# Where a pooled branch is split into high and low parts: in SBUF by two engines, or as it leaves PSUM and by way of HBM

## The chip, the cores and the metric

The kernel runs on one core of a Trainium2 chip. The metric is the device time in microseconds (us) of one execution. TensorE (PE) multiplies matrices and writes to PSUM, VectorE (DVE) and ScalarE (ACT) work on tiles in SBUF and PSUM, GpSimd (POOL) on tiles in SBUF; SyncE (SP) does no arithmetic and starts transfers. A transfer can be started from SP's queue or from POOL's.

## What is computed

One block of a streaming encoder over 16 meta tokens and 1024 tokens of width 1024. Of the reference, what matters here:

```python
a, q, k, v, r, lr, ga, gb = jnp.split(rmsnorm(h, norm_mix) @ w_in, IN_SPLITS, axis=-1)
p = multiscale_pool(a).reshape(B, L, 4, 128)            # trailing means of 2, 4, 8, 16 tokens, less the token
p = jnp.einsum('blgc,gce->blge', p, w_pool_mix).reshape(B, L, 512) * pool_scale
y_a = p @ w_pool_out                                    # 512 -> 1024
log_a = log_sigmoid(lr @ w_gate_up + b_gate) / 16       # lr: 16 columns
o = gla_chunked(q, k, v, log_a)                         # chunks of 64 tokens, 4 heads, state 64 x 128
y_b = (rmsnorm(o) * silu(r)) @ w_gla_out
h = h + (sigmoid(ga) * y_a + sigmoid(gb) * y_b) @ w_out
h = h + squared_relu_mlp(rmsnorm(h))                    # 1024 -> 4096 -> 1024, then a last rmsnorm
```

## The kernel before

All products are float32. A float32 matrix is kept as two float32r parts: the high part is a rounded copy, the low part is the matrix less its high part. `mm3` (L251) then issues three matmuls, high by high (L255), high by low (L256) and low by high (L257). Activations lie transposed, channels on the partitions and tokens along the free axis, in two halves of 512 tokens; `TH[h]` and `TL[h]` are the high and low parts of the normalised input of half h. Weights come through rings of slots: `W1` (L59 to L89) loads 512 KB of raw weights from HBM by SP (L110), ACT writes the high part (L83) and `W1.eng` the low part (L87). That engine is DVE at first and POOL from `gla_open` on, where a slot is split in four quarters of 256 columns.

The stages, with their times in the profiled execution: the gates and other projections up to 245 us, the pooling stage 245 to 304 us, the GLA stage 304 to 475 us, then the merge and `w_out`, then the MLP to the end.

**Pooling stage.** For each of four groups g of 128 channels, `a_block` projects the input, `mean_block` (L892) takes the trailing means on DVE and splits them (high by ACT L904, low by DVE L905), and `mix_block` (L909) multiplies by `w_pool_mix` and has ACT (L915) scale the result from PSUM into a float32 tile `pm` of all 1024 tokens. The steps stand in a list (L965): a of the next group stands between the mean and the mix of one. Then come the queries read back from HBM, the first block of keys `k_block(0)`, the mix of group 0, and `load_vw(1)`, which fetches and splits the second half of the weights of v (high ACT L471, low POOL L474).

**GLA stage.** `gla_open` (L988) gives SBUF and PSUM a new layout and calls `lr_of(0)`, which builds the stacked low-rank rows of the first half: a memset by POOL (L542), copies by ACT (L545) and a difference by DVE (L546), all in `stacked`. The stage walks through four units (token half, head pair): (0,0), (1,0), (0,1), (1,1). A unit starts with its log decay (L1180: PE L1183, ACT L1184 to L1187, DVE L1188), goes on to the running products (DVE L1261 to L1276, ACT L1254, L1257, L1273) and inside scores (PE L1240, L1243), and ends in `across` (L1310): PE L1329 multiplies keys by values, DVE L1335 chains eight states one after the other (W, last S) from these, PE L1342 and L1352 multiply into the states, PE L1370 transposes back. Between the pieces of a unit a list of fill work is poured into PE: k, v, the last two gate blocks, then the pooled product `ya_block` (L938) and the output product of the GLA branch. ya needs the pooled tile in two parts: `pooled_parts` (L1035), run during gate block 7 (`gb_last`, L1047), writes them over `TH[1]` and `TL[1]`, since block 7 is the last reader of these: 8 copies by ACT (L1041), 16 differences by POOL (L1043). Its eight steps come with the eight k steps of block 7's second token half. A gate block runs its halves in the order 1, 0, and a sigmoid of a half is ACT L923 to L925 and L1063 with DVE L926 in the middle.

**What sets the order.** PE's program is written by hand (L1803). The order of ACT, DVE, POOL and SP in these two stages is chosen by a scheduler that looks at the costs the program names; the engine then runs its queue strictly in order. A tile's next writer waits for its last reader.

Of the kernel before, what the change touches and what calls it, by code (L numbers as in the profile page):

```python
# [114 lines left out]
def kernel(  # L115
# [49 lines left out]
    q_dram = dp.tile([2, 2, P, HALF], F32, name="q_dram")  # L165
    r_dram = dp.tile([HEADS, 2, P, HALF], F32, name="r_dram")
    h_dram = dp.tile([8, P, D], F32, name="h_dram")
    hf_dram = [dp.tile([NPAIR, P, HALF], F32, name=f"hf{m}_dram") for m in range(7)]

    ident = left.push("ident", [P, P], F32)  # L170
# [256 lines left out]
    def drive(steps):  # L427

        for ring, aps, fn in steps:
            if fn not in (start, gate_stage):  # L430
                for r in rings:
                    r.top_up()
            wbs = [ring.views.pop(ring.done + ring.kept + i) for i in range(len(aps))] if ring else []
            held = len(aps)
            for cost in fn(*wbs) or ():
                if cost == "free":
                    ring.done, held = ring.done + held, 0
                    for r in rings:
                        r.top_up()
                elif cost == "keep":  # L440
                    ring.kept, held = ring.kept + held, 0
                else:
                    yield cost
            if ring:
                ring.done += held
# [19 lines left out]
    def load_vw(i, raws=None, parts=False):  # L465
        vw, raws = S["vw"][i], raws or fetch_vw(i)
        c = [slice(j * P, (j + 1) * P) for j in range(2)]
        eng = pool if i else dve

        def hi(j):  # L470
            act.activation(vw[:, 0, :, c[j]], raws[j], ACT.Copy)  # L471

        def lo(j):
            eng.tensor_tensor(vw[:, 1, :, c[j]], raws[j], f32(vw[:, 0, :, c[j]]), ALU.subtract)  # L474

        def lr():
# [383 lines left out]
    def pool_open():  # L860
        left.pop_to(left0)
        S["kq"] = [left.push(f"kq{h}", [P, 2, 2, HALF + OFF[h]], F32) for h in range(2)]
        S["left_k"] = left.mark()
        buffer("a", 2, SEQ + META)
        buffer("s", 2, SEQ + META)
        right.pop_to(0)
        S["vw"].append(right.push("vw1", [P, 2, KT, 256], F32R))
        S["pm"] = right.push("pm", [P, 4, SEQ], F32)
        S["ph"] = right.push("ph", [P, 2, SEQ], F32R)
        mw = S["mw"] = right.push("mw", [P, 2, 4, P], F32R)  # L870
        r = raw.load(w_pool_mix.rearrange("g c e -> c g e"), 4 * P).rearrange("p (g e) -> p g e", g=4)
# [37 lines left out]
    def mix_block(g):  # L909
        def fn():  # L910
            wb = (S["mw"][:, 0, g], S["mw"][:, 1, g])
            for tag, c in zip(("ms", "ms"), halves()):
                b = bank(tag)
                mm3(b, 1, lambda i: wb, lambda i: (S["ph"][:, 0, c], S["ph"][:, 1, c]))
                act.activation(S["pm"][:, g, c], b, ACT.Copy, scale=pscale[:, g : g + 1])  # L915
                yield

        return fn
# [19 lines left out]
    def ya_block(j):  # L938
        def fn(wb):
            hi, lo = (t.rearrange("p (k c) -> p k c", k=4) for t in wb)  # L940
            ph, pl = S["pm2"]
            for e, (h, c) in ((e, x) for e in range(2) for x in enumerate(halves())):
                b, w = bank("mm"), slice(e * P, (e + 1) * P)
                for k in (3, 2, 1, 0):
                    mm3(
                        b, 1, lambda i: (hi[:, k, w], lo[:, k, w]), lambda i: (ph[:, k, c], pl[:, k, c]),
                        first=k == 3, last=k == 0,
                    )
                    yield 3 * 512 / 2400
# [12 lines left out]
    a_ = lambda g: step(one, a_block(g), W1, [w_cols(C_A + g * P)])  # L962
    p_ = lambda g: step(one, mean_block(g))
    m_ = lambda g: step(one, mix_block(g))
    for f, i in (  # L965
        (a_, 3), (p_, 3), (a_, 2), (m_, 3), (p_, 2), (a_, 1), (m_, 2), (p_, 1), (a_, 0), (m_, 1), (p_, 0),
    ):
        f(i)

# [9 lines left out]
            for p in range(2):  # L979
                nc.sync.dma_start(q[:, p], q_dram[p, h])  # L980

    step(one, queries)
    step(one, k_block(0), W1, [w_cols(C_K)])
    m_(0)
    step(one, lambda: load_vw(1))


    def gla_open():  # L988
        raw.back()
        W1.eng = pool  # L990
        right.pop_to(2)
        left.pop_to(S["left_k"])
        S["v"].append(left.push("v1", [P, NC, 2 * P], F32))
        buffer("t1", 3)
# [22 lines left out]

    def v_second():
# [5 lines left out]
            leave()  # L1024

    def yg_open():
        S["yg"] = {0: S["vw"][1].rearrange("p n k c -> p (n k c)").rearrange("p (n h c) -> p n h c", n=2, h=HEADS)}

    def yg_last():
        right.pop_to(1)  # L1030
        S["yg"][1] = right.push("yg1", [P, 2, HEADS, HALF], F32R)
        done.add("pm")

    def pooled_parts():


        S["pm2"] = [a[1].rearrange("p k c -> p (k c)").rearrange("p (g c) -> p g c", g=4) for a in (TH, TL)]
        for c in halves():
            for g in (3, 2, 1, 0):
                (ph, pl), pm = (a[:, g, c] for a in S["pm2"]), S["pm"][:, g, c]  # L1040
                act.activation(ph, pm, ACT.Copy)  # L1041
                for q in halves_of_half:
                    pool.tensor_tensor(pl[:, q], pm[:, q], f32(ph[:, q]), ALU.subtract)  # L1043
                yield

    def gb_last(d):
        def fn(wb):  # L1047
            parts = pooled_parts()
            for n, cost in enumerate(gb_block(d, MAIN[::-1])(wb)):
                if n >= KT:  # L1050
                    next(parts, None)
                if n in (KT, KT + 1):
                    gate_load()
                yield cost

        return fn


    def gb_block(d, pieces=MAIN):
# [6 lines left out]
        return lambda wb: project(wb, pieces, evac)  # L1066

    staged = {}

# [240 lines left out]
    def across(p, half):  # L1310
# [38 lines left out]
        for j in (3, 0, 1, 2):  # L1349
            for e, u in ((0, 0), (1, 0), (1, 1), (0, 1)):  # L1350
# [493 lines left out]
```

## Time and profile before

| what | value |
|---|---|
| median of 3 executions | 1222.09 us (1220.26 to 1222.21) |
| the profiled execution | 1217.61 us |
| its span, from the first instruction to the last | 1215.8 us |
| PE busy | 1191.6 us, 98% of the span |
| VectorE busy | 869.7 us, 72% |
| ScalarE busy | 626.3 us, 52% |
| GpSimd busy | 75.0 us, 6% |
| granted TensorE clock | 0.998 |
| moved by DMA | 173.85 MB, 143 GB/s over the span |

A row of the timeline gives a start and a duration in us, the engine, the line, the operation, the tile written and the tiles read, shapes and a count; behind it in brackets how long the engine had been idle and what released it. Several like instructions in a row are one row, with the time of all. The list of waits gives for an engine what it waited for, in total, how often, and the longest. PE's matmuls overlap: one of 512 columns is shown at some 0.39 us and the next begins 0.23 us later.

### The profile page before, as it was taken

How to read it: one execution, taken by the hardware profiler on the slowest of the kernel's cores; microseconds unless marked ns; L12 is line 12 of the kernel's file. 1: busy time of each engine (PE TensorE's matmuls, PEld its weight loads, DVE VectorE, ACT ScalarE, POOL GpSimd, SP SyncE). 2: the span in 40 equal slices, each digit the busy share in tenths (PEclk: the TensorE clock that was granted, in tenths of full speed). 3: DMA queues.
4: the chain of work that ended last, by engine and by line, in shares of the span. 5: the costliest groups of instructions: out<-in, count | busy, mean ns of one | idle time of the engine just before them, and what ended most of it. 6: DMA issues, size and time to landing. Idle time of an engine off the chain costs nothing.

```text
span 1215.8 us, 18356 instructions
## 1 busy us (share of the span) xinstructions
PE 1191.6 (98%) x6794; PEld 993.0 (82%) x6794; DVE 869.7 (72%) x1432; ACT 626.3 (52%) x1123; POOL 75.0 (6%) x112
## 2 busy tenths in 40 slices
PE   7999999999998999999999999999999999999997
PEld 7878888898887877888878888888888888888886
DVE  7996677654666777735897667676675887887686
ACT  7667567744547423324655555454554444444554
POOL 2000000001106216000000000000000000000000
PEclk9999999999999999999999999999999999999999
DMA  8043433431102567741245444454479973333532
GB/s 255 2 113 115 126 95 100 150 94 53 37 19 79 193 200 241 282 133 75 100 139 173 145 159 156 130 169 146 162 237 322 340 243 96 95 97 95 173 96 87
DMA packets 141673, 173.85 MB, mean 143 GB/s; under 512 B 9944, under 2 KB 81392, under 8 KB 141584
## 3 DMA queue, kind: packets, MB, share of 16 engines
q1 hardware_dynamic: 141552, 172.62, 44.1%
q8 instruction: 53, 0.87, 0.3%
q14 instruction: 36, 0.29, 0.1%
q0 software_dynamic: 32, 0.07, 0.1%
HBM read 119.17 MB, written 53.48 MB: 142 GB/s over the span
## 4 chain that ended last, share of the span: by engine, by line
PE 85%; DVE 8%; ACT 3%; DMA 2%; issue 1%; SPq 0%; POOL 0%; DVEq 0%; POOLq 0%; ACTq 0%
PE b_mm L255 10%; PE b_mm L257 9%; PE b_mm L256 9%; PE b_ms L256 9%; PE b_ms L255 9%; PE b_ms L257 9%; PE b_x L256 8%; PE b_x L255 8%; PE b_x L257 8%; PE b_sc L1240 1%; PE b_mx L255 1%; PE b_mx L257 1%; PE b_mx L256 1%; DVE w1l L274 1%; DVE ut L783 1%
## 5 line engine op out<-in xcount | busy, mean ns | idle before, releaser
L255 PE MATMUL b_mm<-th,w1h 128*128 128x512 f32 (+1 forms) x308 | 116.2, 377 | 1.5 <-DVE c L818 1.0
L257 PE MATMUL b_mm<-th,w1l 128*128 128x512 f32 (+1 forms) x308 | 114.2, 371 | 0.0
L256 PE MATMUL b_mm<-tl,w1h 128*128 128x512 f32 (+1 forms) x308 | 114.2, 371 | 0.0
L255 PE MATMUL b_x<-th,w1h 128*128 128x512 f32 (+1 forms) x264 | 100.2, 380 | 0.0
L256 PE MATMUL b_x<-tl,w1h 128*128 128x512 f32 (+1 forms) x264 | 100.1, 379 | 0.0
L257 PE MATMUL b_x<-th,w1l 128*128 128x512 f32 (+1 forms) x264 | 99.7, 378 | 0.0
L273 ACT ACTIVATE w1h<-raw 128x512 fp32r<-128x512 f32 x98 | 60.7, 620 | 28.4 <-PE b_ms L256 13.6
L273 ACT ACTIVATE w1h<-fs 128x512 fp32r<-128x512 f32 x78 | 49.0, 630 | 48.4 <-PE b_ms L256 34.1
L274 DVE TENSOR_TENSOR w1l<-raw,w1h 128x512 fp32r<-128x512 f32 x98 | 67.0, 684 | 8.7 <-ACT w1h L273 8.7
L255 PEld LDWEIGHTS b_mm<-th,w1h 128*128 128x128 f32 x308 | 57.8, 188 | 13.1 <-issue 2.7
L257 PEld LDWEIGHTS b_mm<-th,w1l 128*128 128x128 f32 x308 | 57.8, 188 | 10.2
L256 PEld LDWEIGHTS b_mm<-tl,w1h 128*128 128x128 f32 x308 | 57.8, 188 | 9.4
L274 DVE TENSOR_TENSOR w1l<-fs,w1h 128x512 fp32r<-128x512 f32 x78 | 53.4, 686 | 16.3 <-ACT w1h L273 16.2
L273 ACT ACTIVATE w1h<-bt 128x512 fp32r<-128x512 f32 x44 | 27.8, 632 | 66.9 <-issue 62.7
L257 PEld LDWEIGHTS b_x<-th,w1l 128*128 128x128 f32 x264 | 49.7, 188 | 9.5
L255 PEld LDWEIGHTS b_x<-th,w1h 128*128 128x128 f32 x264 | 49.5, 188 | 9.5
L256 PEld LDWEIGHTS b_x<-tl,w1h 128*128 128x128 f32 x264 | 49.6, 188 | 9.3
L1692 DVE TENSOR_TENSOR bt<-w,w 128x512 f32<-128x512 f32 x80 | 54.7, 684 | 2.0 <-DMA w<-in_w_ff_dram 2.0
L273 ACT ACTIVATE fxh<-bt 128x512 fp32r<-128x512 f32 x36 | 22.8, 632 | 56.0 <-issue 50.4
L273 ACT ACTIVATE w1h<-rawx 128x512 fp32r<-128x512 f32 x44 | 27.5, 629 | 44.2 <-PE b_x L256 18.6
L257 PE MATMUL b_ms<-wo,w1l 128*128 128x512 f32 x128 | 49.9, 390 | 0.0
L255 PE MATMUL b_ms<-wo,w1h 128*128 128x512 f32 x128 | 49.8, 389 | 0.0
(455 smaller groups left out, 3346.8 us busy)
## 6 DMA issues: line engine op xcount, KB each, us to landing
hf_dram<-h SPq DMA_DIRECT2D x112, 256.0 KB, 2.1
raw<-hf_dram SPq DMA_DIRECT2D x112, 256.0 KB, 2.6
w<-in_w_ff_dram SPq DMA_DIRECT2D x64, 256.0 KB, 4.8
raw<-in_w_in_dram SPq DMA_DIRECT2D x22, 512.0 KB, 4.2
raw<-in_w_ff_dram SPq DMA_DIRECT2D x16, 512.0 KB, 4.1
rawx<-in_w_ff_dram SPq DMA_DIRECT2D x16, 512.0 KB, 4.1
rawx<-in_w_in_dram SPq DMA_DIRECT2D x10, 512.0 KB, 4.2
xs<-in_x_dram SPq DMA_DIRECT2D x8, 512.0 KB, 5.4
```

The lines of the kernel that those rows point to most:

```text
L255: pe.matmul(ps, ah, bh, start=first and i == 0, stop=False, skip_group_check=more)
L256: pe.matmul(ps, ah, bl, start=False, stop=False, skip_group_check=more)
L257: pe.matmul(ps, al, bh, start=False, stop=last and i == n - 1, skip_group_check=more)
L273: act.activation(hi, a, ACT.Copy)
L274: dve.tensor_tensor(lo, a, f32(hi), ALU.subtract)
L783: dve.tensor_tensor(to_, a_, b_, ALU.subtract)
L1240: pe.matmul(b[to, e, j], kk[r, s], qq[r, s], start=True, stop=True, tile_position=(e * CH, u * CH))
L1692: dve.tensor_tensor(bt, w, S["w2"][q[3:]][:, i], ALU.add if q[2] == "+" else ALU.subtract)
```

## The change

Five things change.

1. `mix_block` splits the scaled group as it leaves PSUM. ACT writes the high part (L921), DVE the low part from the same PSUM bank (L922, `b x scale - high`). Both go to HBM by SP into `pm_dram`, in 16 stores of 256 KB. `pm` becomes a ring of three slots.
2. `pooled_back` loads the pooled parts of all groups into `TH[1]` and `TL[1]` with four transfers of 1 MB (2048 float32 per partition) from POOL's queue, in place of the 8 copies and 16 differences. The destination is float32r.
3. The last two gate blocks run as a pair, by halves: block 6 half 1, block 7 half 1, block 6 half 0, block 7 half 0. The pooled loads follow the second of these; the slots of the weights come free one at a time.
4. `load_vw(1)` moves ahead of the mean of group 0, and its low parts go from POOL to DVE.
5. The layout of the GLA stage, `lr_of(0)` and the queries move ahead of `k_block(0)` (`gla_first`). The tile `pm` no longer has to be freed inside the stage, and the wait on it in `across` goes.

```diff
+    pm_dram = dp.tile([2, 2, P, 4, HALF], F32, name="pm_dram")
...
+                elif cost == "one":
+                    ring.done, held = ring.done + 1, held - 1
+                    for r in rings:
+                        r.top_up()
...
     def load_vw(i, raws=None, parts=False):
-        eng = pool if i else dve
         def lo(j):
-            eng.tensor_tensor(vw[:, 1, :, c[j]], raws[j], f32(vw[:, 0, :, c[j]]), ALU.subtract)
+            dve.tensor_tensor(vw[:, 1, :, c[j]], raws[j], f32(vw[:, 0, :, c[j]]), ALU.subtract)
...
-        S["pm"] = right.push("pm", [P, 4, SEQ], F32)
+        S["pm"], S["npm"] = right.push("pm", [P, 2, 3, HALF], F32R), 0
...
     def mix_block(g):
-            for tag, c in zip(("ms", "ms"), halves()):
-                b = bank(tag)
+            for h, c in enumerate(halves()):
+                b = bank("ms")
                 mm3(b, 1, lambda i: wb, lambda i: (S["ph"][:, 0, c], S["ph"][:, 1, c]))
-                act.activation(S["pm"][:, g, c], b, ACT.Copy, scale=pscale[:, g : g + 1])
+                hi, lo = (S["pm"][:, n, S["npm"] % 3] for n in range(2))
+                S["npm"] += 1
+                act.activation(hi, b, ACT.Copy, scale=pscale[:, g : g + 1])
+                dve.scalar_tensor_tensor(lo, b, pscale[:, g : g + 1], f32(hi), ALU.mult, ALU.subtract)
+                for n, a in enumerate((hi, lo)):
+                    nc.sync.dma_start(pm_dram[n, h, :, g], f32(a))
...
-        (a_, 3), (p_, 3), (a_, 2), (m_, 3), (p_, 2), (a_, 1), (m_, 2), (p_, 1), (a_, 0), (m_, 1), (p_, 0),
+        (a_, 3), (p_, 3), (a_, 2), (m_, 3), (p_, 2), (a_, 1), (m_, 2), (p_, 1), (a_, 0), (m_, 1), (v_, 1), (p_, 0),
...
-    step(one, queries)
-    step(one, k_block(0), W1, [w_cols(C_K)])
-    m_(0)
-    step(one, lambda: load_vw(1))
-    def gla_open():
+    def gla_first():
         raw.back()
-        W1.eng = pool
-        right.pop_to(2)
         left.pop_to(S["left_k"])
...
+        S["lr"] = left.push("lr", [P, HALF], F32R)
+        S["y"] = left.push("y", [P, HALF], F32)
+        lr_of(0)
+        queries()
+    def gla_open():
+        W1.eng = pool
+        right.pop_to(1)
...
-        S["y"] = left.push("y", [P, HALF], F32)
-        S["lr"] = left.push("lr", [P, HALF], F32R)
-        lr_of(0)
         banks(keep=1, sc=1, m2=1, mx=1, ms=1)
         rota["mm"] = ("mm", "mm", "mx")
+    step(one, gla_first)
+    step(one, k_block(0), W1, [w_cols(C_K)])
+    m_(0)
     step(one, gla_open)
...
-    def pooled_parts():
-        S["pm2"] = [a[1].rearrange("p k c -> p (k c)").rearrange("p (g c) -> p g c", g=4) for a in (TH, TL)]
-        for c in halves():
-            for g in (3, 2, 1, 0):
-                (ph, pl), pm = (a[:, g, c] for a in S["pm2"]), S["pm"][:, g, c]
-                act.activation(ph, pm, ACT.Copy)
-                for q in halves_of_half:
-                    pool.tensor_tensor(pl[:, q], pm[:, q], f32(ph[:, q]), ALU.subtract)
-                yield
+    def pooled_back():
+        S["pm2"] = [a[1].rearrange("p k c -> p (k c)").rearrange("p (h g c) -> p h g c", h=2, g=4) for a in (TH, TL)]
+        for h in range(2):
+            for n in range(2):
+                pool.dma_start(S["pm2"][n][:, h], pm_dram[n, h])
...
+    def gb_pair(d):
+        def fn(*wbs):
+            for half, at, n in MAIN[::-1]:
+                for u in range(2):
+                    yield from gb_block(d + u, [(half, at, n)], False)(wbs[u])
+                    if u and half:
+                        pooled_back()
+                    elif not half:
+                        yield "one"
+            gate_load()
+            gate_load()
...
-    step(fill, gb_block(6), W1, [w_cols(C_GB + 6 * P)])
-    step(fill, gb_last(7), W1, [w_cols(C_GB + 7 * P)])
-    step(fill, yg_last)
+    step(fill, gb_pair(6), W1, [w_cols(C_GB + d * P) for d in (6, 7)])
...
-        while ("pm" if half else "v") not in done:
+        while "v" not in done:
             yield 1.0
```

PE's queue holds the same 6152 instructions in the same order; only what some of them wait for differs. The first place is ACT's queue where the pooling stage meets the GLA stage. `kq` are the keys, `metab` the decay of the meta tokens, `b_ms` a PSUM bank, `small` the pool scales. Before:

```order
L83 ACTIVATE w1h<-raw_115 128x1024
L972 ACTIVATE kq_2237<-b_x 128x512
L915 ACTIVATE pm<-b_ms,small 128x512 x2
L545 ACTIVATE lr<-gB 16x512 x2
L1184 ACTIVATE metab<-b_mm,small 128x16
L1264 ACTIVATE f<-kq_2233 128x256x2
```

And ACT's queue at the same place after:

```order
L83 ACTIVATE w1h<-raw_120 128x1024
L982 ACTIVATE kq_2238<-b_x 128x512
L921 ACTIVATE pm<-b_ms,small 128x512 x2
L1186 ACTIVATE metab<-b_mm,small 128x16
L1266 ACTIVATE f<-kq_2234 128x256x2
```

The two copies into `lr` are gone from here; they stand some forty rows earlier, among the sigmoids of the gates. On DVE the low part L922 of the last group stands where the difference L546 into `lr` stood, and PE's first matmul of the GLA stage, which writes a new bank over the one that L921 and L922 read, waits for that L922 instead of for `lr`.

The second place is POOL's queue in the GLA stage; `w1l` are low parts of weights. Before:

```order
L542 MEMSET lr 80x512
L87 TENSOR_TENSOR w1l<-raw_119,w1h 128x256 x4
L1043 TENSOR_TENSOR tl_143<-pm,th_139 128x256 x16
L87 TENSOR_TENSOR w1l<-raw_115,w1h 128x256 x4
L87 TENSOR_TENSOR w1l<-raw_119,w1h 128x256 x4
```

And after:

```order
L87 TENSOR_TENSOR w1l<-raw_116,w1h 128x256 x4
L546 MEMSET lr 80x512
L1045 DMA tl_144<-pm_dram 128x2048
L1045 DMA th_140<-pm_dram 128x2048 x2
L1045 DMA tl_144<-pm_dram 128x2048
L87 TENSOR_TENSOR w1l<-raw_120,w1h 128x256 x4
```

The four transfers stand ahead of the split of ya's first weights (`raw_120`); before, that split stood ahead of all sixteen differences.

The third place is DVE's queue in the unit (0,1), between the log decay and the state chain; `t` is the sigmoid of a gate, `ends` the decays at the chunks' ends, `n` and `f` running products. Before:

```order
L1272 TENSOR_TENSOR n_2809<-n_2805,mix 128x128x2x2
L926 SCALAR_TENSOR_TENSOR t_2772<-b_mx,t_2772 128x512
L1276 TENSOR_TENSOR ends<-mix 128x256
L1276 TENSOR_TENSOR ends<-ends 128x128
L1274 TENSOR_TENSOR f<-n_2805,mix 128x128x4
L1276 TENSOR_TENSOR ends<-ends 128x64
L1276 TENSOR_TENSOR ends<-ends 128x32
L1276 TENSOR_TENSOR ends<-ends 128x16
L1335 SCALAR_TENSOR_TENSOR W<-S,ends,b_m_3784 128x128
```

And after:

```order
L1274 TENSOR_TENSOR n_2847<-n_2843,mix 128x128x2x2
L1278 TENSOR_TENSOR ends<-mix 128x256
L1278 TENSOR_TENSOR ends<-ends 128x128
L1278 TENSOR_TENSOR ends<-ends 128x64
L1278 TENSOR_TENSOR ends<-ends 128x32
L1278 TENSOR_TENSOR ends<-ends 128x16
L935 SCALAR_TENSOR_TENSOR t_2694<-b_mx,t_2694 128x512
L1276 TENSOR_TENSOR f<-n_2843,mix 128x128x4
L1337 SCALAR_TENSOR_TENSOR W<-S,ends,b_m_3806 128x128
```

The sigmoid's step (L926 before, L935 after) and the product into `f` have moved behind the five steps into `ends`. The state chain starts behind the same work in both, and the lines of the GLA stage stand two further on after the change (L1335 is L1337).

More of the change, by code (lines that the diff above doesn't have):

```diff
@@ L941, in fn @@
             ph, pl = S["pm2"]
-            for e, (h, c) in ((e, x) for e in range(2) for x in enumerate(halves())):
+            for e, h in ((e, h) for e in range(2) for h in range(2)):
                 b, w = bank("mm"), slice(e * P, (e + 1) * P)
@@ L945, in fn @@
                     mm3(
-                        b, 1, lambda i: (hi[:, k, w], lo[:, k, w]), lambda i: (ph[:, k, c], pl[:, k, c]),
+                        b, 1, lambda i: (hi[:, k, w], lo[:, k, w]), lambda i: (ph[:, h, k], pl[:, h, k]),
                         first=k == 3, last=k == 0,
@@ L964 @@
     m_ = lambda g: step(one, mix_block(g))
+    v_ = lambda i: step(one, lambda: load_vw(i))
     for f, i in (
-        (a_, 3), (p_, 3), (a_, 2), (m_, 3), (p_, 2), (a_, 1), (m_, 2), (p_, 1), (a_, 0), (m_, 1), (p_, 0),
+        (a_, 3), (p_, 3), (a_, 2), (m_, 3), (p_, 2), (a_, 1), (m_, 2), (p_, 1), (a_, 0), (m_, 1), (v_, 1), (p_, 0),
     ):
@@ L1026, in yg_open, with gb_block @@
     def yg_open():
[L1027 to L1032, printed above, removed]
-    def pooled_parts():
-        S["pm2"] = [a[1].rearrange("p k c -> p (k c)").rearrange("p (g c) -> p g c", g=4) for a in (TH, TL)]
-        for c in halves():
-            for g in (3, 2, 1, 0):
-                (ph, pl), pm = (a[:, g, c] for a in S["pm2"]), S["pm"][:, g, c]
-                act.activation(ph, pm, ACT.Copy)
-                for q in halves_of_half:
-                    pool.tensor_tensor(pl[:, q], pm[:, q], f32(ph[:, q]), ALU.subtract)
-                yield
[L1046 to L1054, printed above, removed]
+        right.pop_to(0)
+        S["yg"] = {h: right.push(f"yg{h}", [P, 2, HEADS, HALF], F32R) for h in (1, 0)}
+    def pooled_back():
[14 more added lines that the diff above has]
+            gate_load()
         return fn
-    def gb_block(d, pieces=MAIN):
+    def gb_block(d, pieces=MAIN, free=True):
         def evac(b, half, at, n):
@@ L1064, in evac @@
             nc.sync.dma_start(gb_dram[d, half], o)
-        return lambda wb: project(wb, pieces, evac)
+        return lambda wb: project(wb, pieces, evac, free=free)
     staged = {}
```

## The prediction

> **What bounds the kernel now.** I read the busy times first, then what PE waited for, then the timeline around the two long waits, then the rows by slices and the transfers.
>
> ```profile
> PE 1191.6 (98%) x6794; PEld 993.0 (82%) x6794; DVE 869.7 (72%) x1432; ACT 626.3 (52%) x1123; POOL 75.0 (6%) x112
> PE b_x L668 <- DMA ident<-in_ident_dram: 4.7, 1, 4.7
> PE b_m L1342 <- DVE S L1335: 3.5, 1, 3.5
> PE b_ms L1183 <- DVE lr L546: 2.5, 1, 2.5
> PE b_ms L578 <- DVE us L660: 1.2, 2, 1.0
> ```
>
> PE is busy for 1191.6 of 1215.8 us. The change leaves PE's instructions and their order as they are, so the time can move only through PE's waits. Of these (total, count, longest) 4.7 us are the first load, which the change doesn't touch. The next two are in its region: 3.5 us for the last state `S`, 2.5 us for the low-rank rows `lr`. No other wait is above 1.2 us. Together 6.0 us, 0.49% of the time, is the most that can be gained; what can be lost is not bounded this way.
>
> The profiled execution took 1217.61 us, 1.8 us more than its span, and 4.5 us less than the median of 1222.09. I work out the sum as a difference in the profiled execution and put it on the median.
>
> **The seam at 304 us (low-rank rows early; low parts at PSUM).** PE, then ACT and DVE there:
>
> ```profile
> 306.86 0.47 PE L1183 MATMUL b_ms<-lr,wgu 80*128 80x512 f32 x1 [2.49 <-DVE lr L546]
> 304.25 1.26 ACT L915 ACTIVATE pm<-b_ms,small 128x512 f32<-128x512 f32 x2
> 305.39 1.26 ACT L545 ACTIVATE lr<-gB 16x512 fp32r<-16x512 f32 x2
> 306.03 0.68 DVE L546 TENSOR_TENSOR lr<-gB,lr 16x512 fp32r<-16x512 f32 x1 [0.91 <-ACT lr L545]
> 392.77 0.68 DVE L926 SCALAR_TENSOR_TENSOR t<-b_mm,t 128x512 f32<-128x512 f32 x1
> ```
>
> ACT ends the two scalings at 304.25 + 1.26 = 305.51, then makes `lr`, DVE ends it at 306.71, and PE goes on at 306.86. In the changed kernel `lr` is made some 60 us earlier and this wait goes. Late next is the new low part L922 of the last group: PE's first matmul of the GLA stage writes over the bank that it reads. L922 can start when ACT has written the second high part, 305.51. The trace has no L922; the nearest row is the same operation with one operand in PSUM, L926 at 0.68 us. So the bank comes free at 305.51 + 0.68 = 306.19, and with the 0.15 us between DVE's end and PE's start before, PE goes on at 306.34. That gains 306.86 - 306.34 = **0.5 us**, not 2.5. The bounds: nothing, if the first L922 delays the second by another 0.5; 2.49 us, if nothing were left of the wait. I take 0.5, the value from the rows.
>
> **The pooling stage (8 low parts more on DVE, 2 moved from POOL, 16 stores on SP).** 8 x 0.68 = 5.4 us and two splits of 1024 columns at 1.23 us (L87 below, same shape on DVE) come to 7.9 us of DVE in 59 us. Where a mean could become late, before group 0's mix:
>
> ```profile
> 291.21 1.23 DVE L87 TENSOR_TENSOR w1l<-raw,w1h 128x1024 fp32r<-128x1024 f32 x1 [2.58 <-ACT w1h L83]
> 295.60 1.29 DVE L905 TENSOR_TENSOR ph<-s,ph 128x512 fp32r<-128x512 f32 x2 [0.76 <-ACT ph L904]
> 302.83 0.39 PE L255 MATMUL b_ms<-ph,mw 128*128 128x512 f32 x1
> ```
>
> The last mean is split at 295.60 + 1.29 = 296.89, 5.9 us before PE reads it at 302.83. What can fall into DVE's queue ahead of it since the mean before is two low parts and two splits at most, 2 x 0.68 + 2 x 1.23 = 3.8 us. POOL's two splits leave, which can only help DVE. So I take **nothing**: the projection of the next group and the keys hide it. Without that cover it would cost at most the 7.9 us of DVE. The stores are 16 x 256 KB = 4 MB in 59 us, 71 GB/s on top of the 94 and 53 of these slices; the same core reaches 340 GB/s (row of slices below, 30.4 us each). SP's queue is passed by the stores, each of which waits for its part, but weights are fetched a slot ahead; nothing taken, and the 3.8 us above as bound.
>
> **The wait for `S` at 389 us (pooled parts no longer made here).** DVE in the unit (1,0), at which POOL does nothing:
>
> ```profile
> 341.65 0.69 DVE L1274 TENSOR_TENSOR f<-n,mix 128x512 f32<-128x512 f32 x1
> 342.72 0.99 DVE L1276 TENSOR_TENSOR ends<-ends 128x128 f32<-128x128 f32 x4
> 345.63 0.35 DVE L1335 SCALAR_TENSOR_TENSOR W<-S,ends,b_m 128x128 f32<-128x128 f32 x1 [0.79 <-PE b_m L1329]
> 349.76 0.35 DVE L1335 SCALAR_TENSOR_TENSOR S<-W,ends,b_m 128x128 f32<-128x128 f32 x1
> ```
>
> And ACT, POOL, DVE and PE in the unit (0,1), where PE waits:
>
> ```profile
> 376.17 0.62 ACT L1041 ACTIVATE th<-pm 128x512 fp32r<-128x512 f32 x1
> 377.21 0.62 ACT L1186 ACTIVATE mix<-mix 128x512 f32<-128x512 f32 x1
> 376.01 4.67 POOL L1043 TENSOR_TENSOR tl<-pm,th 128x256 fp32r<-128x256 f32 x6
> 378.91 1.17 DVE L1188 SCALAR_TENSOR_TENSOR mix<-y,mix 128x512 f32<-128x512 f32 x1 [2.43 <-ACT mix L1187]
> 382.87 8.13 POOL L1043 TENSOR_TENSOR tl<-pm,th 128x256 fp32r<-128x256 f32 x10 [2.19 <-ACT th L1041]
> 382.87 0.69 DVE L926 SCALAR_TENSOR_TENSOR t<-b_mx,t 128x512 f32<-128x512 f32 x1
> 384.56 1.23 DVE L1274 TENSOR_TENSOR f<-n,mix 128x512 f32<-128x512 f32 x1
> 385.71 2.11 DVE L1276 TENSOR_TENSOR ends<-ends 128x64 f32<-128x64 f32 x3
> 387.75 0.33 DVE L1335 SCALAR_TENSOR_TENSOR W<-S,ends,b_m 128x128 f32<-128x128 f32 x1
> 392.23 0.35 DVE L1335 SCALAR_TENSOR_TENSOR S<-W,ends,b_m 128x128 f32<-128x128 f32 x1
> 382.67 1.10 PE L1329 MATMUL b_m<-v,mix 64*64 64x128 f32 x32
> 392.73 1.10 PE L1342 MATMUL b_m<-v,scc 64*64 64x128 f32 x32 [3.47 <-DVE S L1335]
> ```
>
> PE's wait begins at 392.73 - 3.47 = 389.26. The state chain runs from 387.75 to 392.58, 4.83 us; in the quiet unit it took 345.63 to 350.11, 4.48. It could have started when the key products were done, 382.67 + 1.10 = 383.77, but the `ends` came 4 us later. Three things held them: ACT's copies for the pooled parts between the steps of the decay (two, where two starts are 0.52 apart: from 376.17 to 377.21 there are two, 1.04 us); POOL's sixteen differences, beside which DVE's work on SBUF operands alone ran at 1.7 times its usual time and more (L1188 1.17 against 0.69, L1274 1.23 against 0.69, three L1276 2.11 against 0.99 for four), at least 0.48 + 0.54 + 1.12 = 2.1; and L926 and L1274 standing ahead of the `ends`, 0.69 + 0.69. That is 4.5 us, above the 3.47.
>
> All three go, but not all of POOL's load does: the split of ya's first weights moves into their place.
>
> ```profile
> 373.21 2.84 POOL L87 TENSOR_TENSOR w1l<-raw,w1h 128x256 fp32r<-128x256 f32 x4 [38.03 <-ACT w1h L83]
> 378.77 0.58 ACT L923 ACTIVATE t<-b_mx 128x512 f32<-128x512 f32 x1
> 386.43 1.04 ACT L83 ACTIVATE w1h<-raw 128x1024 fp32r<-128x1024 f32 x1
> ```
>
> It ran at 373.21; now ACT's high part stands behind the L923 that began at 378.77, takes 1.04 us as at 386.43, and puts the four quarters (2.84 us) at 380.4 to 383.3, over the `ends`. Without contention the chain starts at 383.8 to 384.0 and ends at 388.4, before 389.26: no wait. With the quarters holding DVE as the differences did, at most 2 us of it, the chain starts at 385.6 and ends at 390.1, and 0.8 us of the wait remain. I take 0.8, since the same pair of engines was seen to slow each other in every overlap above: a gain of 3.47 - 0.8 = **2.7 us**. Bounds: 0 and 3.47.
>
> The Trainium skill (SBUF — State Buffer, section "SBUF: two separate sides") states that DVE and GpSimd share a port pair as an exclusive lock, which a DVE operation needs when both inputs are in SBUF. The trace agrees, L1274 1.23 us and the PSUM-fed L926 0.69 beside the same POOL work. By that rule one quarter of some 0.7 us at a time blocks, and the wait left would be 0 to 0.8; the sum would be 3.2 to 4.0.
>
> **The four loads from POOL's queue.** No row shows one of 1 MB into float32r. They may start when gate block 7's first half has been read, and ya needs them next:
>
> ```profile
> 366.48 0.39 PE L257 MATMUL b_mm<-th,w1l 128*128 128x512 f32 x1
> 386.37 0.40 PE L255 MATMUL b_mm<-th,w1h 128*128 128x512 f32 x1
> 394.24 0.50 PE L255 MATMUL b_mx<-th,w1h 128*128 128x512 f32 x1
> GB/s 255 2 113 115 126 95 100 150 94 53 37 19 79 193 200 241 282 133 75 100 139 173 145 159 156 130 169 146 162 237 322 340 243 96 95 97 95 173 96 87
> hf_dram<-h SPq DMA_DIRECT2D x112, 256.0 KB, 2.1
> lrraw<-in_w_in_dram POOLq DMA_DIRECT2D x1, 64.0 KB, 5.3
> ```
>
> The block's half ends at 367 to 372 (its last k steps are poured around the transposes that follow 366.48). ya begins at 386.4 with token half 0 and reads half 1 from 394.24 on, about 391 with the wait gone. So 2 MB have 19 us and 4 MB have 391 - 367 = 24 us: 175 GB/s suffice. The slices at 334 to 395 us (the twelfth and the thirteenth) move 19 and 79 GB/s, and the core reaches 340. At 340 the 4 MB take 12 us. From below, by the 64 KB row alone, 5.3 us for so little says nothing good; 256 KB in 2.1 us, one at a time, would be 125 GB/s, 34 us, and 10 us late. I take **nothing**, nearer to the slices than to single small transfers, since four large ones stand in the queue together.
>
> The Trainium skill (DMA: Bandwidth & Descriptors, section "Bandwidth") gives 6.15 us for a transfer of 1 MB from GpSimd's queue. Four in a row would be 24.6 us, an estimate, and the sum 0.6 us smaller. No run here shows it yet.
>
> **The rest.** The pair order makes gate block 7's weights due earlier and each half's sigmoid come at another time; the weights were split 38 us before POOL's next work (the idle time in the row at 373.21), so nothing. The wait on `pm` in `across` gates only SP, nothing.
>
> **Sum:** -0.5 - 2.7 = **-3.2 us**, -0.26%. The profiled execution would be 1214.4, the median 1222.09 - 3.2 = 1218.9; I say 1219.0.
>
> **Rivals.**
> - *Both waits go as a whole*: 6.0 us, 1216.1. For it: S can be ready by 388.4. Against it: L922 reads the bank that PE needs. Chance 0.12.
> - *The wait for S stays*: ya's weight split on POOL, and its high part on ACT, hold the `ends` as the differences did, or the change moves work that wasn't the cause; a gain of the seam's 0.5 and up to 1.5 us of the rest, 1220 to 1222, say 1221.3. For it: POOL works over the same DVE work. Against: 2.84 us of POOL instead of 12.8. The change would then not do what it says for PE. Chance 0.28.
> - *Slower: the pooled parts come late.* POOL's queue moves the 4 MB at under 140 GB/s. At 140 they take 30 us from 367, 6 us late at 391, and the time is 1222.09 - 3.2 + 6 = 1224.9; at 125 GB/s 10 us late, 1229. It turns to slower at 4 MB in 24 + 3.2 + 2.4 = 30 us. If POOL could feed the queue only while DVE is idle (busy 20.91 of 30 us below), 12 us would become 12 / 0.30 = 40, 16 us late, 1235. Chance 0.12, of which 0.03 for this last.
> - *Slower: the low parts on DVE make a mean late in the pooling stage*, by up to 3.8 us per group over the margin of 5.9; price 2 to 8 us. Chance 0.04.
>
> ```profile
> 365.00:395.00 30.00, 26.53 (x321) 21.34 (x320) 20.91 (x38) 23.41 (x41) 18.81 (x24) 1.00 0.25 80
> ```
>
> The Trainium skill (SBUF — State Buffer, same section) warns that transfers from GpSimd's queue starve of descriptors while DVE runs operations that hold the shared port. By that rule the third rival's last case holds here; no row of the trace has such a transfer beside DVE work.
>
> **How the numbers follow.** The forecast has 0.44, with its own range 1217.8 to 1219.8. This kernel's measurement can tell about 0.2%, 2.4 us, from no change. Faster by more: 0.40 of the forecast and the first rival, 0.52. Within: the rest of the forecast and the second rival, 0.32. Slower: 0.16. The range holds the forecast, the second rival and half of the first, and the near end of the third: 1216.5 to 1223.5.
>
> **What would show it.** Right: PE's first matmul on `lr` waits about 2.0 us and names DVE L922; the wait at L1344 (L1342 before) is below 1 us; DVE's L1278 and L1276 take 0.2 to 0.7 each where POOL's weight split doesn't run. Wrong: a wait at the first ya matmul on L1045's tiles (386 or 391 us); a wait at the mix of a group; the wait at L1344 of 3 us or more with POOL L87 beside the `ends`.

## The result, and the profile after

The median went from 1221.17 us (four executions, 1219.85 to 1222.21) to 1214.51 us (four, 1214.30 to 1214.80), a ratio of 0.9946 with an interval of 0.9929 to 0.9963: 6.7 us or 0.54% faster. The forecast was 1219.0 with a range from 1216.5, so the direction was right, the forecast gain was less than half of the measured one, and the result lies below the range. But the profiled execution went from 1217.61 to 1214.46, by 3.15 us, where the prediction had worked out 3.2. Twelve further executions of the changed kernel (below) had a median of 1216.19 us beside 1220.15 for the kernel before, a ratio of 0.9972 (0.9962 to 0.9982), 4.0 us. So one pair of kernels gave three differences: 3.15, 4.0 and 6.7 us. That is what had to be explained. One execution below, of the kernel with L922 twice, was in a slow state (1325.17 us at a mean clock of 0.85) and is left out of its median.

What PE waited for after the change, first lines of the list (total, count, longest):

```profile
PE b_x L672 <- DMA ident<-in_ident_dram: 4.8, 1, 4.8
PE b_ms L1185 <- DVE pm L922: 2.1, 1, 2.1
PE b_ms L582 <- DVE us L664: 1.2, 2, 1.0
PE b_mm L256 <- DVE c L822: 1.0, 1, 1.0
PE b_m L1344 <- DVE S L1337: 0.7, 1, 0.7
```

The wait for `lr` is gone and L922, the last low part, has taken its place, 2.1 us instead of 2.5. The wait for `S` is 0.7 instead of 3.5. No new wait above 0.6 us has come. The timeline at the seam (DVE, then PE) and at the state chain (DVE, POOL, PE):

```profile
303.97 1.23 DVE L87 TENSOR_TENSOR w1l<-raw,w1h 128x1024 fp32r<-128x1024 f32 x1 [5.70 <-ACT w1h L83]
305.11 1.40 DVE L922 SCALAR_TENSOR_TENSOR pm<-b_ms,small,pm 128x512 fp32r<-128x512 f32 x2
306.57 0.50 PE L1185 MATMUL b_ms<-lr,wgu 80*128 80x512 f32 x1 [2.13 <-DVE pm L922]
```

```profile
376.88 0.69 DVE L1190 SCALAR_TENSOR_TENSOR mix<-y,mix 128x512 f32<-128x512 f32 x1 [2.25 <-ACT mix L1189]
380.34 0.98 DVE L1278 TENSOR_TENSOR ends<-mix 128x256 f32<-128x256 f32 x1
381.35 2.26 DVE L1278 TENSOR_TENSOR ends<-ends 128x128 f32<-128x128 f32 x4
384.73 0.34 DVE L1337 SCALAR_TENSOR_TENSOR W<-S,ends,b_m 128x128 f32<-128x128 f32 x1
387.49 1.11 DVE L1276 TENSOR_TENSOR f<-n,ends 128x512 f32<-128x512 f32 x1
389.28 0.35 DVE L1337 SCALAR_TENSOR_TENSOR S<-W,ends,b_m 128x128 f32<-128x128 f32 x1
379.75 3.60 POOL L87 TENSOR_TENSOR w1l<-raw,w1h 128x256 fp32r<-128x256 f32 x4 [6.45 <-ACT w1h L83]
387.31 3.25 POOL L87 TENSOR_TENSOR w1l<-raw,w1h 128x256 fp32r<-128x256 f32 x4 [3.96 <-PE b_mm L258]
382.45 1.10 PE L1331 MATMUL b_m<-v,mix 64*64 64x128 f32 x32
389.77 1.10 PE L1344 MATMUL b_m<-v,scc 64*64 64x128 f32 x32 [0.73 <-DVE S L1337]
```

L1190 runs at its usual 0.69 us; the five L1278 beside POOL's weight split take 0.98 and 2.26 us where the quiet unit had 0.42 for the first (L1276 at 342.26 before) and 0.99 for the other four. The state chain starts at 384.73, 1.18 us after the key products (L1331) are done at 383.55; before, that gap was 387.75 - 383.77 = 3.98 us. And the four loads: POOL's instructions with their starts, then the median time from issue to landing.

```profile
366.62 0.64 POOL L1045 DMA_DIRECT2D tl<-pm_dram  x1 [31.63 <-PE b_mm L258]
367.26 0.56 POOL L1045 DMA_DIRECT2D th<-pm_dram  x1
372.24 0.53 POOL L1045 DMA_DIRECT2D th<-pm_dram  x1 [4.42 <-PE b_mm L258]
372.75 0.55 POOL L1045 DMA_DIRECT2D tl<-pm_dram  x1
```

```profile
tl<-pm_dram POOLq DMA_DIRECT2D x2, 1024.0 KB, 7.2
th<-pm_dram POOLq DMA_DIRECT2D x2, 1024.0 KB, 7.5
```

They land some 7.5 us after they are issued (the median of each pair), where 19 us were to be had.

### The profile page after: what moved, and what is told of

The parts are those of the page before. It is cut to its first block, busy times and chain, and to the rows that moved or that the text cites. A ratio compares the mean times of both kernels' runs of the same rounds, so it can differ in the third digit from the quotient of the medians.

```text
span 1212.7 us, 18406 instructions
## 1 busy us (share of the span) xinstructions
PE 1191.4 (98%) x6794; PEld 993.0 (82%) x6794; DVE 875.3 (72%) x1442; ACT 623.4 (51%) x1115; POOL 60.3 (5%) x98
## 4 chain that ended last, share of the span: by engine, by line
PE 85%; DVE 8%; ACT 3%; DMA 2%; issue 2%; SPq 0%; POOL 0%; DVEq 0%; ACTq 0%; POOLq 0%
PE b_mm L256 10%; PE b_mm L258 9%; PE b_mm L257 9%; PE b_ms L258 9%; PE b_ms L256 9%; PE b_ms L257 9%; PE b_x L257 8%; PE b_x L256 8%; PE b_x L258 8%; PE b_sc L1242 1%; PE b_mx L256 1%; PE b_mx L258 1%; PE b_mx L257 1%; DVE w1l L275 1%; DVE ut L787 1%
```

## The experiments

### Where do the 2 to 5 us come from that the profiled execution of before lacks?

**The kernel before once more**, unchanged. 

> The kernel before, unchanged, run and profiled once more. The profiled executions of before and after differ by 3.15 us (1217.61 and 1214.46), which is the sum that was forecast, but the medians differ by 6.7 us, since the timed executions of before lie 2.2 to 4.6 us above its profiled one. Theory A: the kernel before has a wait that comes out longer in most executions than in the profiled one, in the region of the change (VectorE beside GpSimd in the GLA stage, or the low-rank rows at the seam). Then its times spread over 1217 to 1222 again, and a profile above 1219 shows the excess in the waits for S (over 3.5 us) or for lr (over 2.5 us). Theory B: the excess has nothing to do with the change; then a profile above 1219 shows it elsewhere (the start, the MLP, many small waits), with 3.5 and 2.5 us at those two places as before.

Measured: 1219.84 us (12 executions, 1218.58 to 1222.77), the kernel before beside it 1220.56 (29, 1217.28 to 1222.63), ratio 0.9994 (0.9985 to 1.0003). This time the profiled execution was one of 1222.77 us. Its list of waits:

```profile
PE b_m L1342 <- DVE S L1335: 3.5, 1, 3.5
PE b_ms L1183 <- DVE lr L546: 2.5, 1, 2.5
```

Both waits are what they were in the execution of 1217.61: theory A as stated falls, the waits are not longer. The rows by stretches show what differs. A row gives a stretch of time, its length, the busy time (and number) of PE's matmuls, of its weight loads, of DVE, ACT and POOL, and then PE's granted clock (1.00 is full), the DMA share and GB/s; first the execution of 1217.61, then that of 1222.77:

```profile
308.00:312.00 4.00, 4.00 (x35) 4.00 (x34) 2.15 (x11) 3.37 (x9) 0.00 (x0) 1.00 0.14 42
396.00:400.00 4.00, 4.00 (x76) 3.23 (x75) 1.55 (x3) 1.56 (x3) 0.00 (x0) 1.00 1.02 362
```

```profile
308.00:309.00 1.00, 1.00 (x6) 1.00 (x6) 0.00 (x0) 1.00 (x5) 0.00 (x0) 0.50 1.01 306
311.00:312.00 1.00, 1.00 (x8) 1.00 (x8) 0.94 (x4) 0.00 (x0) 0.00 (x0) 0.82 0.00 0
392.00:396.00 4.00, 1.21 (x24) 1.24 (x28) 3.90 (x9) 0.46 (x1) 4.00 (x5) 0.66 0.02 4
396.00:400.00 4.00, 4.00 (x54) 3.40 (x47) 2.18 (x5) 0.81 (x2) 0.26 (x1) 0.50 0.67 211
400.00:401.00 1.00, 1.00 (x6) 0.55 (x5) 0.00 (x0) 0.00 (x0) 0.00 (x0) 0.95 0.84 289
```

PE is busy all the time from 308 on, but at half its clock until about 311.4, and again until 400.1: just behind the two waits, and nowhere else until PE's last matmul. Two stretches of work at half speed, of 3.4 and 5.3 us, lose half of that, some 4.3 us, most of the 5.2 between the two executions; the other 0.8 us were not traced. The 32 matmuls of L1342 behind the wait for `S` are shown at 1.98 us instead of 1.10. Theory B falls too: the excess stands right behind the waits that the change shortens. This gave theory G: a wait of PE can be followed by a few us at half clock.

**The seam alone** (part 5; `lr_of(0)`, layout and queries ahead of `k_block(0)`):

```diff
-    def gla_open():
+    def gla_first():
...
+        lr_of(0)
+        queries()
+    step(one, gla_first)
     step(one, k_block(0), W1, [w_cols(C_K)])
```

> The kernel before with part 5 alone: the low-rank rows, the layout of the GLA stage and the queries ahead of the first block of keys; the pooled scaling stays on ScalarE into float32, POOL keeps its splits. If the seam is as the prediction has it, PE's first matmul on lr then waits only for ScalarE's second scaling (it ends at 305.5, and PE started 0.15 us after its releaser before), so it starts at 305.7 instead of 306.9: the wait falls from 2.5 to about 1.3 us and the kernel is 1.2 us faster in the profiled execution, with the wait for S unchanged at 3.5. Rival: the variable part of the kernel before lies at the seam; then the median falls by 3 us or more and the executions agree within 0.5 us.

Measured: the wait fell to 1.2 us, for ScalarE's L915, and the profiled execution took 1216.79, 0.8 us less. The median is 1219.52 (1216.79 to 1220.94), ratio 0.9992 (0.9983 to 1.0002). So the wait moved as forecast, but the time followed by less than the 1.2 us expected: behind the seam stand small new waits (0.4 us for `metab`, 0.3 us for `scc`). The spread stays, and the wait for `S` is still 3.5.

**GpSimd's differences left out** (no_pool_lo):

```diff
                 act.activation(ph, pm, ACT.Copy)
-                for q in halves_of_half:
-                    pool.tensor_tensor(pl[:, q], pm[:, q], f32(ph[:, q]), ALU.subtract)
```

> The kernel before with the 16 differences of GpSimd for the pooled low parts left out (the second matmul of the pooled product then reads the old low parts of the input, so the output isn't the reference's); ScalarE's copies stay, and VectorE's queue in the unit (0,1) is the same as before. If GpSimd's work slowed VectorE, as the prediction has it, L1188, L1274 and the L1276 run at 0.69, 0.69 and 0.99 for four, 2.1 us of the wait for S go and it falls to 1.0 to 1.4 us. Rival: ScalarE's copies and the two VectorE steps ahead of the ends are the cause; then the wait stays at 2.5 to 3.5 us. If theory A holds with GpSimd as its cause, the executions also agree within 0.5 us and the median falls by 5 us.

Measured: the wait for `S` fell from 3.5 to 0.7 us, further than the 1.0 to 1.4 expected, the median to 1216.39 (1216.20 to 1217.71), ratio 0.9970 (0.9958 to 0.9981). VectorE in this kernel:

```profile
380.49 0.69 DVE L1186 SCALAR_TENSOR_TENSOR mix<-y,mix 128x512 f32<-128x512 f32 x1 [2.42 <-ACT mix L1185]
385.33 0.69 DVE L1272 TENSOR_TENSOR f<-n,mix 128x512 f32<-128x512 f32 x1
385.93 0.66 DVE L1274 TENSOR_TENSOR ends<-ends 128x64 f32<-128x64 f32 x3
386.50 0.34 DVE L1333 SCALAR_TENSOR_TENSOR W<-S,ends,b_m 128x128 f32<-128x128 f32 x1
```

The first three are the lines that took 1.17, 1.23 and 2.11 us before. From the last step of the decay (L1186 here, L1188 before) to the start of the state chain VectorE takes 6.01 us instead of 8.84. GpSimd's work alone explains 2.8 us of the wait, with ScalarE's copies and VectorE's order as they were. Five of the six executions agree within 0.43 us, yet the profiled one (1216.63) still has the clock at half behind the seam, where the wait is 2.5 as ever:

```profile
308.00:312.00 4.00, 4.00 (x22) 4.00 (x22) 2.04 (x10) 2.60 (x7) 0.00 (x0) 0.57 0.15 46
392.00:396.00 4.00, 4.00 (x92) 3.26 (x85) 2.89 (x6) 1.26 (x2) 0.36 (x1) 1.00 0.60 201
```

**The low parts of v on VectorE** (`eng = dve` in `load_vw`). 

> The kernel before with half of part 4 alone: the low parts of the second half of the weights of v on VectorE instead of GpSimd, at the same place in the program. The prediction took nothing for it: profiled execution 1217.6 plus or minus 0.3, both long waits unchanged. Rival: GpSimd's two splits of 2.4 us beside VectorE's work in the pooling stage are where most executions of the kernel before lose 2 to 4 us; then the median falls by that much and the executions agree within 0.5 us.

Measured: 1219.87 us (1218.57 to 1222.15), ratio 0.9999 (0.9989 to 1.0009), both waits unchanged: nothing in the median, as predicted, and the rival falls. The profiled execution took 1221.62 and not the 1217.6 expected of it: it is one with the clock at half behind both waits.

### Does the clock follow the wait?

**The changed kernel in more executions.** 

> The changed kernel as it is, in more executions. What the first runs showed: the kernel before has the same waits in a 1217.6 us and a 1222.8 us execution (2.5 and 3.5 us), but in the slow one PE's granted clock is 0.50 for 3.4 us right after the wait for lr and for 5 us right after the wait for S. Theory G: a wait of PE of some length makes the clock fall to half for a few us; the price is then the wait plus 1.7 to 2.6 us, in some executions or all. In the changed kernel the two waits are 2.1 and 0.7 us. If 2.1 us is too short for it, all executions lie within 1214.0 to 1215.0. If it depends on where the wait falls in time, some of them lie near 1216.2. Rival theory L: the clock falls for reasons of its own, unrelated to PE's waits; then the changed kernel has executions near 1217 to 1219 too.

Measured: 1216.19 us; two executions at 1214.52 and 1214.57, ten from 1215.66 to 1217.27. The profiled one (1217.27) has the same waits, 2.1 and 0.7, and half the clock behind the first:

```profile
308.00:312.00 4.00, 4.00 (x23) 4.00 (x22) 1.91 (x10) 2.23 (x6) 0.00 (x0) 0.58 0.77 234
```

By time and mean clock the fall is in 9 of these 12 executions, so 2.1 us can be enough. The four with which the result was measured had none of it: 1214.51 is the kernel without the fall, 1216.2 the one with it. No run shows why all four lay on one side.

**No wait at the seam** (ms_first, the bank of the decay first):

```diff
-        banks(keep=1, sc=1, m2=1, mx=1, ms=1)
+        banks(keep=1, ms=1, sc=1, m2=1, mx=1)
```

> The changed kernel with the PSUM banks of the GLA stage laid out in another order (the bank of the decay first instead of last), so that PE's first matmul on lr writes over a bank that was read out earlier, by the copy of the keys, and not over the one that the last low part reads. PE's order is the same. The wait of 2.1 us at the seam then falls to 0.1 to 0.3 us, and the kernel is 1.8 to 2.1 us faster than the changed one: 1212.4 to 1212.7, with all executions within 0.5 us of each other (theory G: no wait over 1.2 us but the first load is left). Rival: the work on ScalarE and VectorE behind the seam is the bound there; then PE waits as long a few us later and the time is that of the changed kernel, 1214.5.

Measured: 1212.48 us (1211.61 to 1212.87), ratio 0.9943 (0.9929 to 0.9957) to the kernel before. PE's matmul on `lr` follows without a wait and the clock stays at 1.00:

```profile
304.74 0.50 PE L1185 MATMUL b_ms<-lr,wgu 80*128 80x512 f32 x1
```

Against the changed kernel's 1216.19 the 2.1 us of wait are worth 3.7. The executions spread over 1.3 us, where 0.5 was expected.

**A longer wait at the seam**: L922 of the last half two and three times.

```diff
+                for _ in range(2 if (g, h) == (0, 1) else 1):
                 dve.scalar_tensor_tensor(lo, b, pscale[:, g : g + 1], f32(hi), ALU.mult, ALU.subtract)
```

> The changed kernel with the last low part L922 computed twice (the same values), so that the wait at the seam is 0.7 us longer: 2.8 to 2.9 us. If a wait costs its length: 1215.2 us, all executions alike. Theory G: the clock also falls to 0.50 for some 3.4 us behind the wait in most executions, as in the kernel before with 2.5 us, and the median is 1.5 to 2 us higher: 1216.5 to 1217.2, with some near 1215.2.

> The changed kernel with the last low part L922 computed three times, so that the wait at the seam is 3.5 to 3.6 us, as long as the wait for S in the kernel before. If a wait costs its length: 1215.9 us. Theory G: the clock falls in nearly all executions, for 3.4 to 6 us at 0.50, and the median is 1217.5 to 1219.

Measured: waits of 3.0 and 3.8 us, medians of 1216.81 and 1217.96 (the trace puts the waits down to small steps on `metab` that VectorE runs beside the repeated L922):

```profile
307.81 0.76 PE L1186 MATMUL b_ms<-lr,wgu 80*128 80x512 f32 x1 [3.00 <-DVE metab L1191]
308.46 0.76 PE L1186 MATMUL b_ms<-lr,wgu 80*128 80x512 f32 x1 [3.79 <-DVE metab L1201]
```

In the second no execution was below 1216.94, while 1214.5 + 1.7 = 1216.2 would be the wait's length alone. In the profiled execution of the first the clock is at half already when PE starts (its first matmul on `lr` is shown at 0.76 us instead of 0.50) and stays there for 6 us. Judged by time and mean clock, there is no sign of a fall in the 6 executions without a wait at the seam; it is in 9 of the changed kernel's last 12 at 2.1 us (9 of 16 with the four of the result), in 10 of 11 at 3.0 and in all 12 at 3.8. So with the wait's length the clock seems to fall more surely.

**The wait for S alone** (the kernel before with the early rows and the bank order of ms_first). 

> The kernel before with the early low-rank rows and the other bank order: the seam is gone (wait 0.1 to 0.3 us), the wait for S stays at 3.5 us, the pooled parts are made by ScalarE and GpSimd as before. Without a fall of the clock 1217.6 - 2.4 = 1215.2 us. Theory G: behind the wait for S the clock falls to 0.50 for some 3.4 to 5 us in most executions, since 3.5 us is longer than any wait that showed it so far but one, so that the median is 1217 to 1218 and the executions spread from 1215 to 1218.5. Rival: the fall of the clock at 395 us needs the earlier one at 308; then all executions lie at 1215.2.

Measured: 1218.72 us (1218.33 to 1220.04), ratio 0.9989 (0.9980 to 0.9998). The wait for `S` is 3.4 us and the clock 0.60 in 392 to 396 us, with none of it at 308: the fall behind `S` needs no earlier one.

```profile
PE b_m L1343 <- DVE S L1336: 3.4, 1, 3.4
PE b_mm L1214 <- DVE metab L1205: 1.4, 1, 1.4
```

The kernel without a fall wasn't seen. The 1217 to 1218 of theory G was missed by 0.7 us, and my 1215.2 was too low besides: a new wait of 1.4 us (L1214 for `metab`) gives back a part of the seam here.

**A short wait** (the early rows, and no differences on GpSimd). 

> The kernel before with the early low-rank rows and without GpSimd's 16 differences (the output isn't the reference's, as in no_pool_lo). The waits are 1.2 us at the seam and 0.7 us for S. Theory G with a least length between 1.2 and 2.1 us: no execution has the clock fall, all lie at 1217.6 - 1.3 - 2.8 = 1213.5 within 0.6 us. If a wait of 1.2 us is enough in some executions: some lie near 1215.2.

Measured: 1214.59 us (five executions, 1214.43 to 1215.07), ratio 0.9954 (0.9940 to 0.9967), and a clock of 1.00 throughout the profiled one. Waits of 1.2 and 0.7 us bring no fall. The time is 1.1 us above my sum; in the trace half a us of that stands ahead of the seam, and behind it there are new waits of 0.4 us (`scc`) and 0.3 us (`metab`), as in the kernel with the early rows alone.

**A version that is faster than both** (ms_first, and ya's first weights split by VectorE):

```diff
+                        W1.eng = pool if u else dve
                         yield "one"
+                        W1.eng = pool
```

> The changed kernel with the other bank order (ms_first), and the low parts of ya's first weights on VectorE in one instruction of 1.23 us instead of four on GpSimd. If GpSimd's split is what keeps the five steps into ends at 3.2 instead of 1.4 us, they run at 1.4 us, and with 1.2 us more of VectorE's own work the wait for S falls from 0.73 to 0.3 us or nothing: 1211.8 to 1212.4 us. Rival: the split lands between the steps and the state chain and costs VectorE as much as it saves: 0.7 us of wait again, 1212.5.

Measured: 1212.01 us (1211.18 to 1212.29), ratio 0.9931 (0.9919 to 0.9944): 8.0 us less than the 1220.06 of the kernel before beside it. VectorE's split takes 1.22 us, the steps into `ends` their usual time, and PE no longer waits for `S`:

```profile
378.53 1.22 DVE L87 TENSOR_TENSOR w1l<-raw,w1h 128x1024 fp32r<-128x1024 f32 x1
381.40 0.66 DVE L1280 TENSOR_TENSOR ends<-ends 128x64 f32<-128x64 f32 x3
381.98 0.34 DVE L1339 SCALAR_TENSOR_TENSOR W<-S,ends,b_m 128x128 f32<-128x128 f32 x1
387.17 1.10 PE L1346 MATMUL b_m<-v,scc 64*64 64x128 f32 x32
```

The chain starts 0.23 us after the key products are done at 381.75, where the changed kernel had 1.18. The half us to ms_first (1212.48), which was run on another chip, is no larger than the spread of the executions, so the times don't show it; the trace shows the wait gone.

## Why the prediction was wrong

- **The order and the waits** were right. PE's order is the same (6794 matmuls in both traces), the two waits that it named moved and no third came.
- **The seam**: the prediction has a gain of 0.5 us with L922 late next. Measured 2.49 - 2.13 = 0.36. The pair of L922 took 1.40 us and ended at 306.51, 0.3 later than worked out: VectorE's weight split (L87) held the first of them until 305.11, and the first held the second.
- **The pooling stage**: nothing, and nothing it was. PE reads the last mean at 302.90 instead of 302.83.
- **The wait for S**: a gain of 2.7 us with 0.8 us left; measured 2.74 and 0.73. The parts came out otherwise than the sum has them. *ScalarE's copies*: VectorE's last step of the decay starts 6.67 us before the key products are done (376.88 and 383.55) instead of 4.86 (378.91 and 383.77), 1.8 us earlier where the prediction had 1.04. A weight split on ScalarE (L83) moved behind the decay as well, and no run separates it from the copies. *GpSimd's differences*: VectorE's way from that step to the state chain is 8.84 us before, 6.01 without the differences and 7.85 in the changed kernel. So they cost 2.8 us, where the prediction had at least 2.1, and GpSimd's weight split gives 1.8 back, near the 2 us that it allowed. *L926 and L1274 ahead of the `ends`*: nothing, since the chain starts behind the same work in both; the prediction counted 1.4 us for them. The gain is thus 1.8 + 1.0 = 2.8 us, and that no_pool_lo is left with the same 0.73 us is a coincidence. The close hit is in part luck: the chain starts 1.18 us behind the key products instead of the 1.8 worked out, but takes 4.90 us instead of 4.5, because a later weight split at 387.31 slows the product into `f` (1.11 us against 0.68).
- **The four loads**: nothing. They land in 7.5 us, and ya's first matmul doesn't wait; the rival of late pooled parts falls. So does its last case, a queue that is fed only while VectorE is idle, which the prediction said applies here: VectorE was busy for 9.3 of the 15 us from 366 to 381.
- **The step that failed** is the first one: "I work out the sum as a difference in the profiled execution and put it on the median", and with it "together 6.0 us is the most that can be gained". The prediction noted that the profiled execution lay 4.5 us under the median and didn't ask why. A wait here costs its length and then, in most executions, 1.5 to 3.1 us of half clock. The profiled execution of before was one without any, so the 3.56 us between it and the median of the four (1221.17) were missing from the sum. The change cut the wait for `S` below the length at which this happens and left that at the seam above it, so it gains 3.15 us in executions without a fall, 4.0 in the medians of the larger sample, and 6.7 (3.15 and the 3.56) where all four executions of the changed kernel had none. The 3.15 us of the profiled pair agree with the 3.2 worked out because both executions were without a fall, and that was luck. No rival carried this, and so no range did.

The Trainium skill (TensorE: Matmul & The Clock Gate, section "Part 1: The HAM clock gate (the "warmup" mystery)") states that PE's clock is halved after an idle window of about 3.4 us, that the window runs freely and isn't started by the kernel, and that the clock comes back after a busy window. The trace agrees on the half (0.50) and on the window: in the execution of 1222.77 the two stretches end at 311.36 and 400.1 by the rows above, 88.7 us apart, which is 26 times 3.41. It differs on the length: here waits of 2.1 to 2.5 us, shorter than the window, were enough. In no_pool_lo the clock fell at about 308.4, so that of the 3.4 us before it PE had been idle for 2.0.

The traces also list the moments at which the clock changed, and these settle more. In all thirteen profiled executions they are whole multiples of 3.413 us apart (87, 1, 24, 2 and 239 of them in the execution of 1222.77), so that the windows are known even where the clock didn't fall. The clock fell at the end of nine windows while PE had work left, and in these PE had been idle for 1.95, 1.95, 1.97, 2.13, 2.37, 2.48, 2.49, 3.03 and 3.41 us. Of the windows after which it stayed full, one had 2.03 us (in the wait for `S` of the kernel with the seam alone) and no other more than 1.76. In the profiled execution of before a window ended inside each wait, at 305.7 and at 391.0, and cut them into 1.30 and 1.18 us and into 1.76 and 1.71: it shows no fall, though its wait for `S` is as long as a window. The profiled execution of the result was cut in the same way (1.02 and 1.10 us at 305.5), the second profiled execution of the changed kernel was not (2.13 us in one window). After a fall the clock stayed at half for a second window where PE was idle for 0.63 us or more of the next one, and came back where it was idle for 0.41 or less.

So a window mostly idle is enough, and where the windows end decides from execution to execution. This also answers theory L, since each fall in these traces belongs to a wait. It rests on where the windows lie in thirteen traces; no run sets the phase, and the exact share stays open, with 1.95 us that brought a fall and 2.03 that didn't. In the executions without a profile the fall is judged by time and mean clock alone.

## What to carry to other kernels

Price a wait of TensorE by its length and by what it does to the clock: here 2 us and more of idle time cost 1.5 to 3.1 us extra in most executions, and 1.2 us cost nothing extra in five. Look for it in the granted clock of the few us behind each long wait, at a resolution finer than the page's slices. When a profiled execution differs from the median by more than the change is worth, explain that first, with a second profile of the same kernel, since a sum made on one execution holds only for executions of its kind.

## What was not expected of the hardware

Half-clock stretches of 3.4 us show in no line of the page, whose slices of 30 us still print 9, and hardly in the mean clock (0.994 against 0.998 for two of them). GpSimd's work on SBUF slows VectorE's operations between SBUF tiles up to three times (2.11 us for three steps that take 0.66), while those fed from PSUM stay at 0.68 to 0.73 us. Four transfers of 1 MB with a change of type, started from GpSimd's queue while VectorE was busy, landed in 7.2 and 7.5 us (the medians of the two pairs).
